# Seven products on eight column tiles in every second gate-and-up pair, with one weight sum per group formed by an accumulating DMA and one more buffer for raw and split weights

## The chip, the cores and the metric

The kernel runs on one core of one Trainium2 chip. The metric is the device time of one execution in microseconds (us). The engines are TensorE (PE, its weight loads PEld), VectorE (DVE), ScalarE (ACT), GpSimd (POOL) and SyncE (SP), which issues nearly all loads. SBUF is the on-chip memory that tiles live in, PSUM the banks that matmuls add up in.

## The reference

A trunk of two layers on 256 tokens with 2048 features, in float32. Each layer has a block of two gated mixers (a causal convolution and an attention with forget gates), a SwiGLU FFN with 5632 hidden columns, and a gated embedding of the layer:

```python
h = rmsnorm(x, norm_mix_g[i]); proj = h @ w_in[i]
glu_in, q, k, v, f_logit, g_conv, g_attn = jnp.split(proj, split_pts, axis=-1)
y_conv = conformer_conv(glu_in, ...)
log_f = jax.nn.log_sigmoid(f_logit + b_forget[i])
y_attn = forgetting_attention(q, k, v, log_f) @ w_attn_out[i]   # scores + C[t] - C[s], causal softmax
x = x + (sigmoid(g_conv) * y_conv + sigmoid(g_attn) * y_attn) @ w_out[i]
gate, up = jnp.split(rmsnorm(x, norm_ffn_g[i]) @ w_gate_up[i], 2, axis=-1)
x = x + (silu(gate) * up) @ w_down[i]
x = x + sigmoid(rmsnorm(x, norm_ple_g[i]) @ w_ple_gate[i]) * (p[i] @ w_ple_proj[i])
```

After the two layers comes a last rmsnorm. Here C is the running sum of log_f over the tokens.

## The kernel before

**Numbers.** A float32 product is made of three matmuls in fp32r: both operands are split into a rounded part and a remainder, and `Sum.add` (L178, L179, L180) adds rounded x rounded, rounded x remainder and remainder x rounded into one PSUM bank. `split` (L139, L140) makes the two parts of a weight half: ScalarE writes the rounded part `h` (a `wh` buffer), VectorE the remainder `l` (a `wl` buffer). `halves` (L299 to L304) does it for activations.

**Tiles.** Activations lie transposed in 16 column tiles of 128 features by 256 tokens. A weight chunk has 512 columns; it comes in groups of four column tiles, each in two halves of 128 x 1024 (512 KB). `fetch` (L131) loads a half on SP into one of `RAWS` = 7 buffers; `wh` and `wl` have 4 buffers each. One half put through `plain` is 12 matmuls with 512 columns: 2 column tiles x 2 token blocks x 3.

**Seven products.** `fast_chunks` takes two weight chunks together, w1 and w2 (for the FFN gate and up). For its first group (or groups, as many as the list `fast` is long), it does not take the 2 x 2 blocks of tokens and column-tile halves by the eight block products but by seven (a form of Strassen's scheme). The activations' combinations are made once by the class `Fast`, on VectorE, for four column tiles. The weights' combinations are made for each pair, out of the four raw halves a11, a12 (of w1) and a21, a22 (of w2): s3 = a11 + a21, then a21 + a22, a11 + a21 and a12 + a11 in place, by `add` (L245) on VectorE. Each of the seven `product`s splits one raw half and is 6 matmuls. p1, q5, q6 and q7 go to their own banks of the pool `ms`, c11, c12 and c21 are shared with the plain halves. The other groups are plain halves; `go` takes the next of them, and so they stand between the products. When the products that make the `u` tiles are done, u1, u4, u3 and u5 are made from the four `ms` banks on ScalarE and VectorE (L260 to L264), and from then on `go` also runs what waits in `turns`, such as transposing the hidden columns of the pair before (`operand`, L313).

**Where it is used.** There are 24 such pairs a layer: 4 for the branch gates, 2 for the output projection, 10 for gate and up (c = 1 to 10; c = 0 is plain), 6 for the down projection in three parts, and 2 for the embedding's gate. All have one group in seven products. In the FFN `norm.fast` holds one `Fast`, and the groups at column tiles 4, 8 and 12 are plain.

**Order.** The program text is given to a scheduler that sets the order on each engine and gives tiles their buffers; each engine then runs its list in order and waits on semaphores. A raw half is fetched when a raw buffer is given back, a split is made when a `wh` and a `wl` buffer are given back by TensorE.

**Other places.** In the attention's `scores`, C[s] is taken off by matmuls that are added to the q k product: with `nsel`, a stack of eight 128 x 128 matrices with one row of -1 each, against `ch` (the running sums in f32; block 0, L706) or `chs` (their two fp32r parts; block 1, L710 and L711). At the start, `warm` issues 10 f32 matmuls on constants, `load_x` brings the first four column tiles in two loads, and `take(0)` scales and splits all four of them before the first weights are split (L159 to L163). POOL makes constants, fills the convolution's margins (L557) and takes the powers of the norms (L425, L446).

Of the kernel before, what the change touches and what calls it, by code (L numbers as in the profile page):

```python
# [35 lines left out]
WARM = 10  # L36
RAWS = 7
# [8 lines left out]
def trunk(ctx, tc, xT, xR, pT, wI, wF, wC, wA, wOut, wGU, wD, wPG, wPP, vec, bF, gF, out):  # L46
# [5 lines left out]
    whs = pool("whs", 4)  # L52
    wls = pool("wls", 4)
    tmps = pool("tmps", 9)
# [13 lines left out]
    def small(n=2):  # L68
        return keep.tile([P, 16], F32, tag="small", name=f"small{next(uid)}", bufs=12)[:, :n]
# [55 lines left out]
    nsel = const.tile([P, H, P], F32R, tag="nsel", name="nsel")  # L125
# [20 lines left out]
    def fetch_first(src, hook):  # L146

        parts = []
        for half in range(2):
# [3 lines left out]
            c = half * 1024  # L153
            if half == 0:
                for k in range(2):
                    nc.scalar.dma_start(raw[:, k, :], src[:, k * 512 : (k + 1) * 512])
                warm()
                hook()
            else:  # L159
                nc.sync.dma_start(raw.rearrange("p k n -> p (k n)"), src[:, c : c + 1024])  # L160
            for k in range(2):
                act.activation(h[:, k, :], raw[:, k, :], AF.Copy)  # L162
                dve.tensor_tensor(l[:, k, :], raw[:, k, :], h[:, k, :].bitcast(F32), op=ALU.subtract)  # L163
# [50 lines left out]
    def fast_chunks(fast, w1, w2, xs, ks, first, to=None, by_block=None):  # L214
# [32 lines left out]
        for g, f in enumerate(fast):  # L247
            a11, a21 = fetch(w1[g][:, :1024]), fetch(w2[g][:, :1024])
            a22, a12 = fetch(w2[g][:, 1024:]), fetch(w1[g][:, 1024:])
            s3 = raws.tile([P, 2, 512], F32, tag="raw", name=f"sum{next(uid)}")  # L250
            product(p1, f(B11), a11)
            add(s3, a11, a21)
# [5 lines left out]
            product(q6, f(T2), a11)  # L258
            if g == len(fast) - 1:
# [177 lines left out]
    def rstd_c(q):  # L437
# [14 lines left out]
        rb = keep.tile([P, S], F32, tag="rb", name=f"rb{next(uid)}", bufs=1)  # L452
# [13 lines left out]
    def take(q, lo=0, hi=4):  # L466
        for k in range(lo, hi):
            if k % 2 == 0:
                o = pair(F32R)
                norm.tiles[4 * q + k], norm.tiles[4 * q + k + 1] = o[:, 0, :], o[:, 1, :]  # L470
            norm.xs[4 * q + k] = by_blocks(norm.tiles[4 * q + k])
            halves(
                norm.tiles[4 * q + k], xin[q].rearrange("p a b -> p (a b)")[:, k * S : (k + 1) * S],
                norm.gain(4 * q + k),
            )

    load_x(0, 0, 2)
    nc.sync.dma_start(vecs[:, :KD], vec[:, :KD])
# [8 lines left out]
    def hook():  # L487
        load_x(0, 2, 4)
        take(0)
# [9 lines left out]
    def rest(q):  # L499
        def go():  # L500
            take(q)
# [18 lines left out]
    for i in range(L):  # L520
# [61 lines left out]
        wf = keep.tile([P, KD, H], F32, tag="wf", name=f"wf{next(uid)}", bufs=1)  # L582
        nc.sync.dma_start(wf, wF[i].rearrange("p (k h) -> p k h", h=H))
        wfc = keep.tile([P, KD, 2, H], F32R, tag="wfc", name=f"wfc{next(uid)}", bufs=1)
# [3 lines left out]
        ch = keep.tile([P, S], F32, tag="ch", name=f"ch{next(uid)}", bufs=1)  # L588
# [54 lines left out]
        def running_sums():  # L643
# [4 lines left out]
            act.activation(ch, pc[:, :S], AF.Copy)  # L648
            halves(chs, ch)
# [18 lines left out]
        if i == 0:  # L668
            for h in range(H):
                dve.tensor_scalar(nsel[:, h, :], ones, ident[:, h : h + 1], -1.0, op0=ALU.mult, op1=ALU.mult)  # L670
# [24 lines left out]
        def scores(hd):  # L695
            st = {}

            def sc():
                q, kt = qT[hd], kT[hd]
                pr = []  # L700
                for b in range(2):
# [3 lines left out]
                    if b == 0:  # L705
                        pe.matmul(  # L706
                            ps[:, :n], lhsT=nsel[:, hd, :].bitcast(F32), rhs=ch[:, :n], start=False, stop=True
                        )
                    else:
                        pe.matmul(ps[:, :S], lhsT=nsel[:, hd, :], rhs=chs[:, S:], start=False, stop=False)  # L710
                        pe.matmul(ps[:, :S], lhsT=nsel[:, hd, :], rhs=chs[:, :S], start=False, stop=True)  # L711
# [161 lines left out]
        norm = Norm(g_ffn, fast=1)  # L873
# [170 lines left out]
```

## Time and profile before

| | before |
|---|---|
| median of 3 runs | 2839.4 us (2838.63 to 2839.59) |
| the profiled execution | 2838.76 us |
| its span, first to last instruction | 2836.7 us |
| mean granted clock of TensorE | 0.998 |
| matmuls of L178, L179, L180, each | 3552 into `mm`, 416 into `ms` |
| HBM read | 538.91 MB, 191 GB/s over the span |
| raw halves loaded for gate and up | 352 of 512 KB |

Lines of the costliest groups are read so: line, engine, operation, what it writes and reads, shapes, count, then busy time and the mean of one instruction in ns, then the engine's idle time before them and what ended most of it. Names are those of the program with the numbers left out: `raw` and `sum` are raw halves, `wh` and `wl` split ones, `mm` and `ms` PSUM banks, `pair` tiles of activations. A line of the timeline has the start, the length, the engine and the line, and the number of instructions merged into it. A line of the waits has who waited for whom, the sum in us, how often, and the longest.

### The profile page before, as it was taken

What the parts mean: (1) busy time and instruction counts of PE and PEld (TensorE: products, weight loads), DVE (VectorE), ACT (ScalarE), POOL (GpSimd) and SP (SyncE); (2) the same over time, 40 slices, a digit from 0 to 9 for tenths busy, and PEclk for the clock granted to TensorE, in tenths of its full rate; (3) what the DMA queues carried; (4) which work ended last, traced back from release to release, by engine and by line L of the source; (5) the groups of instructions that cost most, each with busy time, mean ns of one, the idle gap of its engine ahead of it and who ended that gap; (6) DMA issues with size and microseconds to landing.
All of it is one profiled execution on the core that took longest, in us unless ns stands there. A gap on an engine that the chain in (4) does not pass through costs nothing.

```text
span 2836.7 us, 34661 instructions
## 1 busy us (share of the span) xinstructions
PE 2816.3 (99%) x12744; PEld 2330.0 (82%) x12744; DVE 2342.3 (83%) x2992; ACT 1560.0 (55%) x1883; POOL 9.9 (0%) x41
## 2 busy tenths in 40 slices
PE   9999999999999999999999999999999999999998
PEld 7888888888888888888788888888888888888886
DVE  6998877868888888888869988678688888888877
ACT  6445745555555545556644466455555555455565
POOL 0000000000000000000000000000000000000000
PEclk9999999999999999999999999999999999999999
DMA  7554555565555556555555545555555556556563
GB/s 284 189 183 156 180 200 193 174 203 186 192 200 202 191 198 202 194 191 199 189 175 188 180 154 190 197 192 178 193 195 194 198 193 210 184 199 207 177 222 128
DMA packets 150074, 543.28 MB, mean 192 GB/s; under 512 B 16912, under 2 KB 17168, under 8 KB 149648
## 3 DMA queue, kind: packets, MB, share of 16 engines
q1 hardware_dynamic: 149040, 539.50, 56.3%
q8 instruction: 99, 1.62, 0.2%
q10 hardware_dynamic: 864, 1.57, 0.2%
q14 instruction: 71, 0.58, 0.1%
HBM read 538.91 MB, written 2.10 MB: 191 GB/s over the span
## 4 chain that ended last, share of the span: by engine, by line
PE 93%; DVE 5%; issue 1%; ACT 1%; DMA 0%; SPq 0%; POOLq 0%; POOL 0%; DVEq 0%; ACTq 0%
PE mm L180 27%; PE mm L179 27%; PE mm L178 27%; PE ms L178 3%; PE ms L180 3%; PE ms L179 3%; DVE wl L140 2%; DVE pair L544 2%; PE ms L313 2%; PE ms L704 0%; ACT wh L139 0%; PE ms L740 0%; DVE raw L245 0%; DMA pair<-in_xT_dram 0%; DVE pair L780 0%
## 5 line engine op out<-in xcount | busy, mean ns | idle before, releaser
L139 ACT ACTIVATE wh<-raw 128x1024 fp32r<-128x1024 f32 x1110 | 1175.9, 1061 | 1113.4 <-PE mm L180 909.5
L140 DVE TENSOR_TENSOR wl<-raw,wh 128x1024 fp32r<-128x1024 f32 x1110 | 1344.2, 1222 | 443.9 <-ACT wh L139 430.1
L178 PE MATMUL mm<-wh,pair 128*128 128x512 f32 x3552 | 1390.4, 392 | 4.2 <-ACT wh L162 2.3
L180 PE MATMUL mm<-wh,pair 128*128 128x512 f32 x3552 | 1384.4, 390 | 0.8 <-DVE pair L301 0.8
L179 PE MATMUL mm<-wl,pair 128*128 128x512 f32 x3552 | 1384.6, 390 | 0.4 <-DVE wl L140 0.3
L180 PEld LDWEIGHTS mm<-wh,pair 128*128 128x128 f32 x3552 | 667.0, 188 | 140.8 <-DVE pair L301 1.7
L178 PEld LDWEIGHTS mm<-wh,pair 128*128 128x128 f32 x3552 | 667.0, 188 | 140.0 <-ACT wh L139 2.7
L179 PEld LDWEIGHTS mm<-wl,pair 128*128 128x128 f32 x3552 | 667.7, 188 | 137.8 <-DVE wl L140 1.3
L544 DVE SCALAR_TENSOR_TENSOR pair<-pair,vecs,pair 128x256 f32<-128x256 f32 x480 | 202.7, 481 | 0.0
L245 DVE TENSOR_TENSOR raw<-raw,raw 128x1024 f32<-128x1024 f32 x144 | 175.9, 1222 | 2.7 <-DMA raw<-in_wD_dram 0.3
L178 PE MATMUL ms<-wh,pair 128*128 128x512 f32 x416 | 162.8, 391 | 1.0 <-ACT pair L975 1.0
L180 PE MATMUL ms<-wh,pair 128*128 128x512 f32 x416 | 162.0, 389 | 0.0
L179 PE MATMUL ms<-wl,pair 128*128 128x512 f32 x416 | 161.9, 389 | 0.0
L178 PEld LDWEIGHTS ms<-wh,pair 128*128 128x128 f32 x416 | 78.1, 188 | 17.9 <-ACT pair L975 1.8
L180 PEld LDWEIGHTS ms<-wh,pair 128*128 128x128 f32 x416 | 78.1, 188 | 16.3
L179 PEld LDWEIGHTS ms<-wl,pair 128*128 128x128 f32 x416 | 78.1, 188 | 16.1
L139 ACT ACTIVATE wh<-sum 128x1024 fp32r<-128x1024 f32 x48 | 50.9, 1061 | 67.0 <-PE mm L180 67.0
L140 DVE TENSOR_TENSOR wl<-sum,wh 128x1024 fp32r<-128x1024 f32 x48 | 58.6, 1220 | 11.6 <-ACT wh L139 11.6
L245 DVE TENSOR_TENSOR sum<-raw,raw 128x1024 f32<-128x1024 f32 x48 | 58.8, 1224 | 2.3 <-DMA raw<-in_wGU_dram 1.0
L288 DVE TENSOR_TENSOR tmp<-mm,tmp 128x512 f32<-128x512 f32 x80 | 51.4, 682 | 2.7 <-PE mm L180 2.7
L245 DVE TENSOR_TENSOR tmp<-tmp,mm 128x512 f32<-128x512 f32 x80 | 51.4, 680 | 0.0
L245 DVE TENSOR_TENSOR tmp<-tmp,ms 128x512 f32<-128x512 f32 x80 | 51.1, 681 | 0.0
(179 smaller groups left out, 1122.8 us busy)
## 6 DMA issues: line engine op xcount, KB each, us to landing
raw<-in_wGU_dram SPq DMA_DIRECT2D x352, 512.0 KB, 4.3
raw<-in_wI_dram SPq DMA_DIRECT2D x287, 512.0 KB, 4.0
raw<-in_wD_dram SPq DMA_DIRECT2D x176, 512.0 KB, 3.9
raw<-in_wOut_dram SPq DMA_DIRECT2D x64, 512.0 KB, 3.7
raw<-in_wPG_dram SPq DMA_DIRECT2D x64, 512.0 KB, 4.2
raw<-in_wA_dram SPq DMA_DIRECT2D x32, 512.0 KB, 4.6
raw<-in_wC_dram SPq DMA_DIRECT2D x32, 512.0 KB, 4.5
raw<-in_wPP_dram SPq DMA_DIRECT2D x8, 512.0 KB, 5.6
```

Source lines behind the costliest of these rows:

```text
L139: act.activation(h, raw, AF.Copy)
L140: dve.tensor_tensor(l, raw, h.bitcast(F32), op=ALU.subtract)
L178: pe.matmul(self.t, lhsT=xh, rhs=wh, start=start, stop=False)
L179: pe.matmul(self.t, lhsT=xh, rhs=wl, start=False, stop=False)
L180: pe.matmul(self.t, lhsT=xl, rhs=wh, start=False, stop=self.left == 0)
L245: add = lambda o, a, b: dve.tensor_tensor(o, a, b, op=ALU.add)
L288: dve.tensor_tensor(u, c.t, u, op=ALU.subtract)
L313: pe.transpose(pt[:, kk * S + b * P : kk * S + (b + 1) * P], src(b)[:, c : c + P], ident)
L544: dve.scalar_tensor_tensor(cv[c], u[c][:, j : j + S], w, cv[c], op0=ALU.mult, op1=ALU.add,)
```

## The change

In the FFN the norm holds two `Fast` operands. A pair with odd c uses both: eight of its 16 column tiles go through seven products, and the groups at 8 and 12 are plain. A pair with even c uses the first only, as before. In all pairs s3 is no longer added on VectorE: a11's half is loaded a second time into s3's buffer, and a DMA issued by POOL adds a21's half from HBM onto it. Inside a group the products and plain halves stand in another order. The raw buffers become 8, the split ones 5 each; to make room, the scratch tiles (`tmps`) become 8 and also hold `wf`, `wfc` and `pin`, and some small tiles share or go.

In `scores`, both blocks use the two fp32r parts `chs`, and the matrix with the row of -1 is one column of a negated identity, `nident`, repeated 128 times in the access pattern; `nsel` and `ch` go. At the start there are 20 warm-up matmuls, the first column tile is loaded by itself, the gains (`vecs`) are loaded by POOL, and each of the first column tiles is scaled just before the weights that it meets are split.

```diff
-WARM = 10
-RAWS = 7
+WARM = 20
+RAWS = 8
...
-    whs = pool("whs", 4)
-    wls = pool("wls", 4)
-    tmps = pool("tmps", 9)
+    whs = pool("whs", 5)
+    wls = pool("wls", 5)
+    tmps = pool("tmps", 8)
...
             for k in range(2):
+                take(0, 2 * half + k)
                 act.activation(h[:, k, :], raw[:, k, :], AF.Copy)
...
             a22, a12 = fetch(w2[g][:, 1024:]), fetch(w1[g][:, 1024:])
-            s3 = raws.tile([P, 2, 512], F32, tag="raw", name=f"sum{next(uid)}")
+            s3 = fetch(w1[g][:, :1024])
+            nc.gpsimd.dma_start(s3.rearrange("p k n -> p (k n)"), w2[g][:, :1024], accum_op=ALU.add)
             product(p1, f(B11), a11)
-            add(s3, a11, a21)
             add(a21, a21, a22)
             product(q5, f(M1), a21)
             go()
             product(q7, f(T3), s3)
             add(a11, a11, a21)
             product(q6, f(T2), a11)
+            product(c21, f(N4X), a22)
+            if len(left) > 2 * len(ks):
+                go()
+            product(c11, f(B21), a12)
+            add(a12, a12, a11)
             if g == len(fast) - 1:
...
                 state["quiet"] = False
-                go()
-            product(c21, f(N4X), a22)
             if len(left) > 2 * len(ks):
                 go()
-            product(c11, f(B21), a12)
-            if g == 0 and len(left) > 2 * len(ks):
-                go()
-            add(a12, a12, a11)
             product(c12, f(B22), a12)
...
-    load_x(0, 0, 2)
-    nc.sync.dma_start(vecs[:, :KD], vec[:, :KD])
+    nc.gpsimd.dma_start(vecs[:, :KD], vec[:, :KD])
+    load_x(0, 0, 1)
...
     def hook():
+        load_x(0, 1, 2)
         load_x(0, 2, 4)
-        take(0)
...
-        wf = keep.tile([P, KD, H], F32, tag="wf", name=f"wf{next(uid)}", bufs=1)
+        wf = tmps.tile([P, KD, H], F32, tag="tmp", name=f"wf{next(uid)}")
...
-            act.activation(ch, pc[:, :S], AF.Copy)
-            halves(chs, ch)
+            halves(chs, pc[:, :S])
...
-                    if b == 0:
-                        pe.matmul(
-                            ps[:, :n], lhsT=nsel[:, hd, :].bitcast(F32), rhs=ch[:, :n], start=False, stop=True
-                        )
-                    else:
-                        pe.matmul(ps[:, :S], lhsT=nsel[:, hd, :], rhs=chs[:, S:], start=False, stop=False)
-                        pe.matmul(ps[:, :S], lhsT=nsel[:, hd, :], rhs=chs[:, :S], start=False, stop=True)
+                    row = nident[:, hd : hd + 1].to_broadcast([P, P])
+                    pe.matmul(ps[:, :n], lhsT=row, rhs=chs[:, S : S + n], start=False, stop=False)
+                    pe.matmul(ps[:, :n], lhsT=row, rhs=chs[:, :n], start=False, stop=True)
...
-        norm = Norm(g_ffn, fast=1)
+        norm = Norm(g_ffn, fast=2)
...
-                    up = fast_chunks(norm.fast, w1, w2, norm.xs, (4, 8, 12), gate)
+                    nf = 1 + c % 2
+                    up = fast_chunks(norm.fast[:nf], w1, w2, norm.xs, (4, 8, 12)[nf - 1 :], gate)
...
-                pin = keep.tile([P, 2, S], F32, tag="pin", name=f"pin{i}", bufs=1)
+                pin = tmp().rearrange("p (k s) -> p k s", k=2)
```

More of the change, by code (lines that the diff above doesn't have):

```diff
@@ L464, in load_x, with take @@
         )
[L466 to L474, printed above, removed]
[L475 to L478 removed]
+    def take(q, k):
+        if k % 2 == 0:
+            o = pair(F32R)
+            norm.tiles[4 * q + k], norm.tiles[4 * q + k + 1] = o[:, 0, :], o[:, 1, :]
+        to = norm.tiles[4 * q + k]
+        halves(to, xin[q].rearrange("p a b -> p (a b)")[:, k * S : (k + 1) * S], norm.gain(4 * q + k))
+        norm.xs[4 * q + k] = by_blocks(to)
+    nc.gpsimd.dma_start(vecs[:, :KD], vec[:, :KD])
+    load_x(0, 0, 1)
     def warm():
@@ L500, in go @@
         def go():
-            take(q)
+            for k in range(4):
+                take(q, k)
             load_x(q + 1) if q < 3 else None
```

16 lines of the change are left out of this document (6 added, 10 removed).

## The prediction

> **What bounds the kernel now.** I read the page first (engine shares, chain, costliest groups), then what TensorE waits for, then one gate-and-up pair of the FFN, where the change puts its new products. All of it is the profiled execution of before: 2838.76 us, of which the span is 2836.7, so 2.1 us lie around it; the median of the runs, 2839.4, is 0.6 higher, and the sum below is made against 2838.8.
>
> ```profile
> span 2836.7 us, 34661 instructions
> PE 2816.3 (99%) x12744; PEld 2330.0 (82%) x12744; DVE 2342.3 (83%) x2992; ACT 1560.0 (55%) x1883; POOL 9.9 (0%) x41
> PE 93%; DVE 5%; issue 1%; ACT 1%; DMA 0%; SPq 0%; POOLq 0%; POOL 0%; DVEq 0%; ACTq 0%
> L139 ACT ACTIVATE wh<-raw 128x1024 fp32r<-128x1024 f32 x1110 | 1175.9, 1061 | 1113.4 <-PE mm L180 909.5
> L140 DVE TENSOR_TENSOR wl<-raw,wh 128x1024 fp32r<-128x1024 f32 x1110 | 1344.2, 1222 | 443.9 <-ACT wh L139 430.1
> L245 DVE TENSOR_TENSOR sum<-raw,raw 128x1024 f32<-128x1024 f32 x48 | 58.8, 1224 | 2.3 <-DMA raw<-in_wGU_dram 1.0
> ```
>
> The reader is to see that the kernel is TensorE's: 99% busy, 93% of the chain. The splitters wait for it and not the other way: ScalarE's rounding (L139) idles 909.5 us for a matmul to give back a split tile, and VectorE's remainder (L140) idles behind that rounding. A busy PE can hide pauses, so its waits and its pace come next.
>
> ```profile
> PE mm L178 <- ACT wh L162: 2.3, 1, 2.3
> PE mm L178 <- ACT wh L139: 1.8, 3, 1.2
> PE ms L485 <- POOL ones L105: 1.2, 1, 1.2
> ...
> 1500.06 0.39 PE L179 MATMUL mm<-wl,pair 128*128 128x512 f32 x1
> ...
> 1501.42 0.39 PE L179 MATMUL mm<-wl,pair 128*128 128x512 f32 x1
> ...
> 694.18:737.26 43.08, 43.08 (x196) 35.74 (x195) 34.67 (x36) 22.73 (x25) 0.00 (x0) 1.00 0.57 195
> 2264.90:2308.00 43.10, 43.10 (x196) 35.76 (x195) 36.84 (x41) 24.55 (x27) 0.00 (x0) 1.00 0.58 193
> ...
> L313 PE MATMUL ms<-ident,tmp 128*128 128x128 f32 x8 | 1.0, 272 | 0.0
> ...
> L261 DVE TENSOR_TENSOR tmp<-tmp,ms 128x512 f32<-128x512 f32 x1 | 0.7, 681 | 0.0
> ```
>
> TensorE's largest waits together are about 5 us, two thirds of that in the first 8 us. From 1500.06 to 1501.42 there are six steps of one matmul: 1.36 / 6 = **0.227 us** for 128x512. A pair before is 186 such matmuls (7 products of 6, 12 plain halves of 12) and 8 transposes of about 1.0 us together: 186 x 0.227 + 1.0 = 43.2 against 43.08 measured from one pair's end to the next. So a pair holds nothing but matmuls, and a matmul taken out is worth its 0.227 us as long as the splits keep up. Columns of the window rows are length, then busy time (and count) of PE, PEld, DVE, ACT, POOL, granted clock, DMA share and GB/s: VectorE has 34.67 to 36.84 us of work in a pair, 80 to 85%.
>
> **The change, part by part.**
>
> *Seven products on eight column tiles, c = 1, 3, 5, 7, 9 of each layer.* The second group of four column tiles costs 7 x 6 = 42 matmuls instead of 4 x 12 = 48. Six saved, ten pairs: 60 x 0.227 = **-13.6 us**. An odd pair should take 43.1 - 1.4 = 41.7 us.
>
> *What the odd pair needs from VectorE.* Three splits more (22 instead of 19) and two additions more (six instead of four, since the sum s3 leaves in both groups): 5 x 1.22 = 6.1 us, so 34.67 + 6.1 = 40.8 to 36.84 + 6.1 = 42.9 us, against 41.7 of TensorE. The even pair loses one addition: 33.4 to 35.6 of 43.1. Over two pairs 74.2 to 78.5 of 84.8 us (88 to 93%). VectorE fits on the mean and is level with TensorE in the odd half, where the fifth wh and wl buffers carry it: I take 0 for stalls. If this cover is gone, the tightest place decides: after the last plain half of the second group come five products back to back, 5 x 1.36 = 6.8 us on TensorE, with five splits, two additions and four updates like L261 (0.68 us) on VectorE, 11.3 us. The 4.5 us difference must come from split tiles made ahead (four ahead, as the next fence shows, and in this stretch worth 1.36 to 2.72 us each). ScalarE gains 3 x 1.06 us in 41.7 and has room.
>
> *The sum s3 by DMA, 58 groups.* Out go 48 additions of 1.22 us on VectorE, which TensorE did not wait for: 0 gained. In come 58 loads on SP and 58 accumulating loads on POOL, 512 KB each: 2 x 58 x 0.524 = 60.8 MB.
>
> ```profile
> 722.58 1.23 DVE L245 TENSOR_TENSOR sum<-raw,raw 128x1024 f32<-128x1024 f32 x1
> ...
> 736.07 1.28 DVE L288 TENSOR_TENSOR tmp<-mm,tmp 128x512 f32<-128x512 f32 x2
> ...
> 738.59 1.22 DVE L140 TENSOR_TENSOR wl<-sum,wh 128x1024 fp32r<-128x1024 f32 x1
> ...
> 736.55 1.06 ACT L139 ACTIVATE wh<-sum 128x1024 fp32r<-128x1024 f32 x1 [1.66 <-PE mm L180]
> ...
> q1 hardware_dynamic: 149040, 539.50, 56.3%
> raw<-in_wGU_dram SPq DMA_DIRECT2D x352, 512.0 KB, 4.3
> pair<-in_xT_dram SPq DMA_DIRECT2D x3, 512.0 KB, 9.6
> ```
>
> Bandwidth holds: 56.3% for 539.5 MB becomes about 63%; an odd pair moves 20 halves, 10.5 MB in 41.7 us, 252 GB/s against 195. What matters is lateness. Today s3's slot is free at 722.58 and its rounding starts at 736.55, when TensorE has just begun the pair (its last result of the pair before is read at 736.07) with four split tiles ahead. In those 14.0 us now go a load (4.3 us) and the accumulating load, so the latter may take 9.7 us before anything is late, and about 15 before TensorE is, as the four tiles ahead hold 1.36 + 1.36 + 2.72 us or more. With eight raws and five split buffers both ends move earlier by about one tile. The second group of an odd pair is tighter: its s3 gets a slot at the split of the second plain half, and from there to its own split lie four products and two halves, 4 x 1.36 + 2 x 2.72 = 10.9 us of TensorE (8 x 1.22 = 9.8 of VectorE). Less 4.3, the accumulating load may take 5.5 to 6.6 us, and about 8 before TensorE stands, since the tiles ahead are also wanted by the five products. No accumulating DMA is in the trace; the nearest rows are 4.3 and, for the slowest transfers of that size, 9.6 us. I take 6, beside the 4.3, because both move the same bytes and only the second reads the tile too: **0**. At 9.6 us it would be (9.6 - 8) x 10 = +16. The page "DMA: Bandwidth & Descriptors" of the Trainium skill, section "Anatomy of one DMA — SWDGE (gpsimd) path", fits a transfer issued by GpSimd by 2.0 us plus bytes over 436 GB/s, an estimate of 3.2 us here; by it the sum would be the same, and no run yet shows it.
>
> *Queues.* SP issues 58 more loads and never leads the chain (SPq 0%). On POOL the powers of the norms and of the convolution's norm (L425, L446) and the memsets of L557 queue behind an accumulating load that waits for its first load. Their readers come a projection or more later, except L446, which a matmul waits for in the background work: 0 to 4.3 us, once a layer; I take **+0.5**.
>
> *Scores.* The f32 matmul pair with nsel in block 0 becomes two fp32r ones with chs; block 1 stays two.
>
> ```profile
> 200.15 0.49 PE L704 MATMUL ms<-pair,pair 128*128 128x128 f32 x2
> 200.47 0.39 PE L706 MATMUL ms<-ch,nsel 128*128 128x128 f32 x2
> 200.69 0.60 PE L704 MATMUL ms<-pair,pair 128*128 128x256 f32 x2
> 200.94 0.47 PE L710 MATMUL ms<-chs,nsel 128*128 128x256 f32 x1
> 201.25 0.28 PE L711 MATMUL ms<-chs,nsel 128*128 128x256 f32 x1
> 201.36 0.39 PE L178 MATMUL mm<-wh,pair 128*128 128x512 f32 x1
> ```
>
> By starts, L706 costs 200.69 - 200.47 = 0.22 us, and the fp32r pair L710, L711 costs 201.36 - 200.94 = 0.42 at twice the columns. The step from fp32r to f32 also costs: L704 takes 0.32 for 128 columns behind fp32r and 0.25 for 256 behind f32, so about 0.1. Per head the rise lies between 0 (half the columns, half the time) and 0.2 + 0.1 = 0.3 us, and 16 heads give 0 to +4.8. As the 0.42 seems to be mostly the change of type and of weights, I take 0.22 a head: **+3.5**.
>
> *Start.*
>
> ```profile
> 1.20 4.44 PE L485 MATMUL ms<-ones 128*128 128x128 f32 x20 [1.20 <-POOL ones L105]
> 7.97 0.73 PE L178 MATMUL mm<-wh,pair 128*128 128x512 f32 x2 [2.33 <-ACT wh L162]
> ...
> 10.56 0.63 PE L178 MATMUL mm<-wh,pair 128*128 128x512 f32 x1
> 10.99 0.63 PE L179 MATMUL mm<-wl,pair 128*128 128x512 f32 x1
> ...
> 5.34 0.91 ACT L303 ACTIVATE pair<-pair,vecs 128x256 fp32r<-128x256 f32 x2 [2.12 <-DMA vecs<-in_vec_dram]
> ```
>
> After the pause from 5.64 to 7.97 the matmuls start 0.43 us apart until about 11.8, some 6 of them, 1.3 us lost. Twenty more warm-up instructions fill that pause. Against it, vecs comes by POOL, behind its memsets, perhaps 2 us later, while ScalarE needs one scaled tile before the first weights instead of four (3 x 0.46 us less). Between -1.5 and +1.7; I take **-0.5**.
>
> *The rest at 0.* The second fast operand of the FFN norm (some 2 us more on each of VectorE and ScalarE, twice) lies beside the second output pair, where two sums leave VectorE. The freed nsel builds were idle filling. The eight tmps now also hold wf, wfc and pin; the slots that these loads need were last read a projection earlier, so SP should not stop. If it did, one load and one split (4.3 + 2.3 us) at four places, 26 us, would show as SP waiting.
>
> *Sum:* -13.6 + 0.5 + 3.5 - 0.5 = -10.1; 2838.8 - 10.1 = **2828.7 us**.
>
> **Rivals.**
>
> *A, the forecast* (2824 to 2833.7): TensorE stays saturated. For it: a pair without a gap, and 88 to 93% on VectorE over two pairs. Against: level loads in the odd pair.
>
> *B, the odd pairs stall*: VectorE becomes the bound in them, or their second s3 is a little late. Each loses 0.5 to 1.6 us, ten times 5 to 16: 2834 to 2845. For it: 42.9 us of VectorE in 41.7, and the 4.5 us at the five products. Against: VectorE idles over 6 us in the pair before.
>
> *C, slower*: the accumulating load takes over 9.6 us behind 250 GB/s of other loads, and TensorE waits for q7 in the second group of every odd pair. From about 9.6 us on the loss passes the gain; at 12 it is (12 - 8) x 10 = +40, 2869; past 15 all 58 groups stall, +58 us for each us. For it: one 512 KB transfer did take 9.6. Against: the median is 4.3 at 57% load. One way to it, 0.04 of C's 0.13: POOL can't prepare the transfer while VectorE is in a long run of splits.
>
> ```profile
> 708.36 4.72 DVE L140 TENSOR_TENSOR wl<-raw,wh 128x1024 fp32r<-128x1024 f32 x4
> ```
>
> With 4.7 us of waiting on top of 6 it takes 10.7: (10.7 - 8) x 10 = +27, 2856. The page "SBUF — State Buffer" of the Trainium skill, section "SBUF: two separate sides", has such a rule, against this change: descriptors of a GpSimd DMA wait while VectorE holds a shared port in a two-port mode. Its section "Who interferes with whom" only infers that an operation on two tensors, as here, leaves the descriptors free; no run here shows either.
>
> *D, better than the sum*: fp32r at 128 columns costs nothing more and the start gains fully: 2838.8 - 13.6 - 1.5 = 2823.7, or a little below as the old waits leave.
>
> **How the numbers follow.** A 0.60, B 0.21, C 0.13, D 0.06. About 0.2%, 5.7 us, is what a measurement of this kernel can tell from no change: faster is below 2833.7, slower above 2845.1. Faster holds A and D, 0.66; within, B, 0.21; slower, C, 0.13. The range takes in A, B and most of D: 2822.5 to 2845.
>
> **What would show it.** Right: 11844 matmuls with 512 columns; odd pairs of 41.7 us and even ones of 43.1 from up's last product to the next; "sum" gone from VectorE; TensorE's waits near 10 us in all; rows of the scores' L710 form at block 0, 0.3 to 0.4 us a pair. Wrong: TensorE waiting for ScalarE's rounding of the sum (C, or late s3), for L140 in odd pairs (B); SP waiting for a tmp; the first 512-column matmul later than 10 us.

## The result

| kernel | median us (range, executions) | against before, 95% interval |
|---|---|---|
| before | 2839.4 (2838.6 to 2839.8, 6) | |
| changed | 2859.8 (2858.4 to 2861.9, 6) | 1.0074 [1.0063, 1.0085] |

The changed kernel is 20.4 us slower; 2828.7 was forecast, and the range ended at 2845. The matmuls are as announced: 60 with 512 columns fewer, 11844. The first view is the page of the changed kernel: spans, engines, queues, the chain of waits, and its costliest groups beside the rows quoted of before (lines moved by one: L140, L141, L246 were L139, L140, L245; the product's matmuls are L179 to L181).

```profile
span 2857.9 us, 34978 instructions
PE 2818.6 (99%) x12704; PEld 2320.6 (81%) x12704; DVE 2350.7 (82%) x3000; ACT 1576.1 (55%) x1916; POOL 60.6 (2%) x100
...
q1 hardware_dynamic: 157392, 569.91, 59.0%
q0 software_dynamic: 8384, 30.42, 6.1%
...
PE 14%; DVE 2%; DMA 1%; issue 1%; ACT 0%; POOLq 0%; POOL 0%; DVEq 0%; ACTq 0%
...
L140 ACT ACTIVATE wh<-raw 128x1024 fp32r<-128x1024 f32 x1188 | 1237.6, 1058 | 1150.8 <-PE mm L181 754.7
L141 DVE TENSOR_TENSOR wl<-raw,wh 128x1024 fp32r<-128x1024 f32 x1188 | 1425.1, 1221 | 427.6 <-ACT wh L140 423.9
...
L246 DVE TENSOR_TENSOR raw<-raw,raw 128x1024 f32<-128x1024 f32 x174 | 212.7, 1222 | 32.9 <-DMA raw<-in_wD_dram 17.1
```

PE is busy 2.3 us more than before with 60 matmuls less. A busy PE holds pauses here: a matmul in front of which weights come late is shown as a longer one (0.50 us instead of 0.39 in the rows of c = 3 below). The 59% of q1 carries 569.9 MB, so 0.104% for each MB; q0, the accumulating transfers that POOL issues, takes 0.20% for each MB (run 4 shows why). The chain's 14% only says that it could be followed back over a small part of the span; it can't be set against the 93% of before. What TensorE and ScalarE wait for in the changed kernel says more (columns: us in total, times, longest):

```profile
PE mm L180 <- DVE wl L141: 10.6, 18, 1.1
PE mm L179 <- ACT pair L303: 5.6, 1, 5.6
...
ACT wh L140 <- DVE raw L246: 140.0, 65, 5.4
...
ACT wh L140 <- DMA raw<-in_wGU_dram: 75.3, 27, 5.4
```

TensorE has two new waits: one of 5.6 us for a scaled activation (the start), and 18 for a remainder. Behind the second stand ScalarE's waits for VectorE's additions (140.0 us, 21.7 before) and, 75.3 us in 27 waits, for weights of gate and up.

For the whole sum I cut both traces at the starts of the 512-column matmuls, counted in program order, and took each stage's length from its first to the next stage's first:

| stage, both layers together | before to changed, us | forecast |
|---|---|---|
| to the end of the first gate projection (end at 97.9, now 105.5) | +7.6 | -0.5 |
| the ten odd pairs | +8.9 | -13.6 |
| the pairs c = 2 | +4.6 | 0 |
| second half of the branch gates, with the scores | +2.3 | +3.5 |
| last part of the down projection | +2.1 | 0 |
| embedding's gate and end | -3.7 | 0 |
| all else | -0.6 | 0 |
| span | +21.2 | |

An odd pair should have lost 1.36 us. None did: the nearest, c = 9 of the first layer, lost 0.9, and c = 3 there went from 42.2 to 44.8 us. So some 22.5 us of stalls (8.9 + 13.6) stand in the odd pairs, and that and the start are the failure.

**One odd pair read closely.** First the source view of L252, the 58 accumulating loads (who waited for them, us, times; then the time to landing). Then, for the second group of c = 3, the transfers' rows, SP's and POOL's, with the median us to landing; and the time lines of SP, POOL, ScalarE, VectorE and TensorE (start, length, engine, line; in brackets the idle time before it and what ended it).

```profile
ACT wh L140: 67.1, 20
...
DMA to landing us min/median/max: 5.6/8.1/9.8
```

```profile
raw<-in_wGU_dram SPq DMA_DIRECT2D x1, 512.0 KB, 5.1
...
raw<-in_wGU_dram POOLq DMA_DIRECT2D x1, 512.0 KB, 9.1
```

```profile
818.93 0.33 SPq L134 DMA_DIRECT2D raw<-in_wGU_dram  x1
...
824.68 0.85 POOL L252 DMA_DIRECT2D raw<-in_wGU_dram  x1 [20.31 <-issue]
...
833.91 2.96 ACT L140 ACTIVATE wh<-raw 128x1024 fp32r<-128x1024 f32 x3 [5.07 <-DMA raw<-in_wGU_dram]
...
835.00 4.63 DVE L141 TENSOR_TENSOR wl<-raw,wh 128x1024 fp32r<-128x1024 f32 x4 [4.90 <-ACT wh L140]
...
835.61 0.39 PE L179 MATMUL ms<-wh,pair 128*128 128x512 f32 x1
836.29 0.50 PE L180 MATMUL ms<-wl,pair 128*128 128x512 f32 x1 [0.29 <-DVE wl L141]
...
842.12 0.50 PE L179 MATMUL mm<-wh,pair 128*128 128x512 f32 x1 [0.29 <-ACT wh L140]
843.38 0.50 PE L180 MATMUL mm<-wl,pair 128*128 128x512 f32 x1 [0.76 <-DVE wl L141]
```

The slot's first load is issued at 818.93 and takes 5.1 us; POOL issues the accumulating load at 824.68, and it lands 9.1 us later at 833.8. ScalarE, which takes its tiles in order, idles 5.07 us in front of it, VectorE then 4.90 us. From 818.93 to 833.8 the sum has taken 14.9 us, where the prediction had worked out 10.9 us between slot and split; in all ten second groups it is 12.9 to 14.9, 14.1 in the median. TensorE runs on from the tiles ahead until 835.6, and then loses 0.45 us, 0.44 us and 1.03 us (steps of 0.68, 0.67 and 1.26 in place of 0.227), 1.9 of the pair's 4.0, of which the rows call only 1.3 idle; most of the rest is one more such step, 1.27 us too long, at 847.7. The 4.9 us that VectorE lost come back as late splits behind the sum, among the products that the prediction had called the tightest place.

### The profile page after: what moved, and what is told of

Read it like the earlier page. It is cut to its first block, busy times and chain, and to the rows that moved or that the text cites. A ratio compares the mean times of both kernels' runs of the same rounds, so it can differ in the third digit from the quotient of the medians.

```text
span 2857.9 us, 34978 instructions
## 1 busy us (share of the span) xinstructions
PE 2818.6 (99%) x12704; PEld 2320.6 (81%) x12704; DVE 2350.7 (82%) x3000; ACT 1576.1 (55%) x1916; POOL 60.6 (2%) x100
## 3 DMA queue, kind: packets, MB, share of 16 engines
q0 software_dynamic: 8384, 30.42, 6.1%
## 5 line engine op out<-in xcount | busy, mean ns | idle before, releaser
L140 ACT ACTIVATE wh<-raw 128x1024 fp32r<-128x1024 f32 x1188 | 1237.6, 1058 | 1150.8 <-PE mm L181 754.7
L141 DVE TENSOR_TENSOR wl<-raw,wh 128x1024 fp32r<-128x1024 f32 x1188 | 1425.1, 1221 | 427.6 <-ACT wh L140 423.9
L179 PE MATMUL mm<-wh,pair 128*128 128x512 f32 x3452 | 1354.1, 392 | 9.4 <-ACT pair L303 5.6
L180 PE MATMUL mm<-wl,pair 128*128 128x512 f32 x3452 | 1348.8, 391 | 11.2 <-DVE wl L141 10.6
L181 PE MATMUL mm<-wh,pair 128*128 128x512 f32 x3452 | 1345.7, 390 | 0.0
L179 PEld LDWEIGHTS mm<-wh,pair 128*128 128x128 f32 x3452 | 648.9, 188 | 144.9 <-ACT wh L140 6.6
L181 PEld LDWEIGHTS mm<-wh,pair 128*128 128x128 f32 x3452 | 648.8, 188 | 135.5 <-DVE pair L304 0.8
L246 DVE TENSOR_TENSOR raw<-raw,raw 128x1024 f32<-128x1024 f32 x174 | 212.7, 1222 | 32.9 <-DMA raw<-in_wD_dram 17.1
L179 PE MATMUL ms<-wh,pair 128*128 128x512 f32 x496 | 194.4, 392 | 2.0 <-ACT wh L140 1.7
L180 PE MATMUL ms<-wl,pair 128*128 128x512 f32 x496 | 193.6, 390 | 1.1 <-DVE wl L141 1.1
L181 PE MATMUL ms<-wh,pair 128*128 128x512 f32 x496 | 193.1, 390 | 0.0
L179 PEld LDWEIGHTS ms<-wh,pair 128*128 128x128 f32 x496 | 93.1, 188 | 23.6 <-ACT wh L140 3.0
L181 PEld LDWEIGHTS ms<-wh,pair 128*128 128x128 f32 x496 | 93.1, 188 | 19.4
L246 DVE TENSOR_TENSOR tmp<-tmp,mm 128x512 f32<-128x512 f32 x80 | 51.9, 680 | 0.0
L246 DVE TENSOR_TENSOR tmp<-tmp,ms 128x512 f32<-128x512 f32 x80 | 51.1, 680 | 0.0
L252 POOL DMA_DIRECT2D raw<-in_wGU_dram x30 | 25.6, 854 | 816.4 <-DVE wl L141 289.2
L399 ACT ACTIVATE tmp<-xt 128x512 f32<-128x512 f32 x56 | 34.8, 623 | 14.1 <-DVE xt L862 8.4
L862 DVE TENSOR_TENSOR xt<-xt,tmp 128x512 f32<-128x512 f32 x64 | 41.1, 684 | 0.0
```

Of the source, the lines that this page charges most:

```text
L140: act.activation(h, raw, AF.Copy)
L141: dve.tensor_tensor(l, raw, h.bitcast(F32), op=ALU.subtract)
L179: pe.matmul(self.t, lhsT=xh, rhs=wh, start=start, stop=False)
L180: pe.matmul(self.t, lhsT=xh, rhs=wl, start=False, stop=False)
L181: pe.matmul(self.t, lhsT=xl, rhs=wh, start=False, stop=self.left == 0)
L246: add = lambda o, a, b: dve.tensor_tensor(o, a, b, op=ALU.add)
```

## The experiments

The theory after this reading: the two transfers of a *second* s3 do not fit into the time between its slot and its split (lateness); and the start is lost to vecs on POOL. The rivals: VectorE's load in the odd pair stalls them whatever s3 does; accumulating as such or POOL hold the engines up; the scores or the new order cost it. The ratio is against before, which was run beside each.

| run | median us | ratio, 95% interval |
|---|---|---|
| vecs_on_sp | 2854.0 | 1.0054 [1.0039, 1.0069] |
| one_fast | 2845.9 | 1.0026 [1.0017, 1.0036] |
| second_sum_on_vector | 2834.7 | 0.9986 [0.9976, 0.9995] |
| plain_on_pool | 2839.6 | 1.0003 [0.9993, 1.0012] |
| vecs_sp_second_vector | 2827.4 | 0.9956 [0.9939, 0.9973] |
| vecs_sp_sum_loaded_first | 2860.4 | 1.0074 [1.0059, 1.0089] |
| vecs_sp_all_sums_vector | 2827.0 | 0.9955 [0.9941, 0.9970] |
| vecs_sp_every_pair | 2834.2 | 0.9986 [0.9976, 0.9995] |
| vecs_sp_second_four_bufs | 2864.6 | 1.0093 [1.0078, 1.0108] |
| vecs_sp_seven_raws | 2910.2 | 1.0258 [1.0241, 1.0276] |
| vecs_sp_all_vector_c1_one | 2824.8 | 0.9951 [0.9934, 0.9967] |

### 1. The start: vecs back on SP

```diff
-    nc.gpsimd.dma_start(vecs[:, :KD], vec[:, :KD])
     load_x(0, 0, 1)
+    nc.sync.dma_start(vecs[:, :KD], vec[:, :KD])
```

> The changed kernel with one line moved: the gains of the first tiles (vecs) are loaded by SP again, behind the first column tile, instead of by POOL. In the changed kernel the first 512-column matmul starts at 14.19 us (7.97 before) and the GLU stage takes 91.3 us (90.0 before), 7.6 us lost together. Theory (the gains' transfer and the place that the scheduler gives to its readers is the whole loss of the start): first matmul near 8 us, 2859.8 - 7.6 = 2852 us. Rival (the split loads, the twenty more warm-up matmuls or the scaling between the splits cost it): first matmul still after 11 us, 2856 us or more. Nothing in the FFN should move.

The transfer's row (KB, us to landing) in the changed kernel, in vecs_on_sp and in before:

```profile
vecs<-in_vec_dram POOLq DMA_DIRECT2D x1, 8.0 KB, 6.5
```

```profile
vecs<-in_vec_dram SPq DMA_DIRECT2D x1, 8.0 KB, 3.3
```

```profile
vecs<-in_vec_dram SPq DMA_DIRECT2D x1, 8.0 KB, 4.0
```

The start of the changed kernel, from the time lines of POOL, ScalarE and TensorE, and a window row (its last three numbers: granted clock, DMA share, GB/s); then of vecs_on_sp:

```profile
2.89 0.74 POOL L474 DMA_DIRECT2D vecs<-in_vec_dram  x1
...
10.21 1.06 ACT L140 ACTIVATE wh<-raw 128x1024 fp32r<-128x1024 f32 x1 [0.18 <-DMA raw<-in_wI_dram]
...
12.68 1.06 ACT L140 ACTIVATE wh<-raw 128x1024 fp32r<-128x1024 f32 x1 [0.18 <-DMA raw<-in_wI_dram]
13.64 1.69 ACT L303 ACTIVATE pair<-pair,vecs 128x256 fp32r<-128x256 f32 x4
...
14.19 0.80 PE L179 MATMUL mm<-wh,pair 128*128 128x512 f32 x1 [5.57 <-ACT pair L303]
...
16.46 0.63 PE L180 MATMUL mm<-wl,pair 128*128 128x512 f32 x1
16.89 0.63 PE L181 MATMUL mm<-wh,pair 128*128 128x512 f32 x1
...
13.70:20.50 6.80, 6.28 (x14) 4.49 (x15) 2.87 (x6) 2.02 (x6) 0.00 (x0) 0.50 1.03 422
```

```profile
4.59 0.51 ACT L303 ACTIVATE pair<-pair,vecs 128x256 fp32r<-128x256 f32 x1 [1.37 <-DMA vecs<-in_vec_dram]
...
7.58 0.48 PE L179 MATMUL mm<-wh,pair 128*128 128x512 f32 x1
7.90 0.39 PE L180 MATMUL mm<-wl,pair 128*128 128x512 f32 x1
8.13 0.40 PE L181 MATMUL mm<-wh,pair 128*128 128x512 f32 x1
```

On POOL the 8 KB land at 9.4 us (2.89 + 6.5). That alone is 4.2 us later than in before (issued at 1.24, 4.0 to landing); the rest is order: on ScalarE the first scaling stands *behind* the roundings of 10.21 to 12.68, of later weights, and starts at 13.64, and TensorE idles 5.57 us. It then runs at steps of 0.43 us (16.46 to 16.89), and the window row says why: the granted clock (the share of its full clock that TensorE gets) is 0.50 from 13.7 to 20.5 us. In before it is 0.50 from 8.7 to 12.1 us, behind a pause of 2.33 us; in vecs_on_sp nowhere at the start. On SP the first product starts at 7.58 and soon runs at 0.23 us a step, and the first projection ends at 96.1 instead of 105.5: 9.4 us. The median moved by 5.8 only, and the span by 2.3: the profiled execution (2857.3) is the slowest of its four, and its odd pairs are 8.3 us longer in sum than the changed kernel's, where nothing in the FFN should have moved. The accumulating transfers are as slow (median 8.2), but load and sum of a second group together take 13.9 to 16.0 us, 15.0 in the median against 14.1; ten times that is about the difference. Why they are slower here stays open.

### 2. Without the second group: one_fast

```diff
-        norm = Norm(g_ffn, fast=2)
+        norm = Norm(g_ffn, fast=1)
...
-                    nf = 1 + c % 2
+                    nf = 1
```

> The changed kernel with seven products on four column tiles in all gate-and-up pairs, as before the change (the FFN norm has one such operand), and everything else of the change kept: sums by DMA, more buffers, scores, start. Theory (late: the second group's sum lands too late in the odd pairs, and its lateness reaches into the pair behind it): all pairs at 43.1 us, the FFN's 15.3 us of loss gone, 2859.8 - 15.3 = 2844.5 us; the first groups' sums never stop TensorE. Rival (the accumulating transfers cost TensorE something everywhere): pairs above 43.3 us and 2850 us or more.

All pairs are as in before to 0.04 us (43.1; 42.2 for c = 3 and 7), although every first group still has its sum by DMA, with a median of 7.9 us to landing. So a sum of 8 us is in time in a first group and too late only in a second one. The median is 6.4 us over before, and the span of the trace 6.8: the start (+6.4), branch gates (+1.0 and +1.4), the last part of the down projection (+0.9) and the embedding's gate (-1.5 and -1.1).

### 3. The second sum on VectorE: second_sum_on_vector

```diff
-            s3 = fetch(w1[g][:, :1024])
-            nc.gpsimd.dma_start(..., w2[g][:, :1024], accum_op=ALU.add)
+            if g == 0:
+                s3 = fetch(w1[g][:, :1024])
+                nc.gpsimd.dma_start(..., w2[g][:, :1024], accum_op=ALU.add)
+            else:
+                s3 = raws.tile([P, 2, 512], F32, tag="raw", name=f"sum{next(uid)}")
             product(p1, f(B11), a11)
+            if g > 0:
+                add(s3, a11, a21)
```

> The changed kernel, but in the second group of the odd gate-and-up pairs (ten groups of 58) the sum s3 is added on VectorE as before the change; all other sums stay by DMA. Theory (late): the accumulating transfer of the second group takes 8.0 to 9.3 us where 5.5 to 6.6 were to spare, and ScalarE idles 3.5 to 5.4 us in front of it; without it odd and even pair together fall from 87.1 to 90.2 us (89.9 in the median of those seen) to about 84.8 to 85.5, and the kernel to 2831 to 2838 us. Rival (work: the odd pair has more splits and additions than VectorE and ScalarE can do): VectorE gets 1.2 us more in each odd pair, so the pairs stay where they are or grow, 2859 us or more.

The windows of the pair c = 3, of the changed kernel and then of this one (length, busy time and count of PE, PEld, DVE, ACT, POOL, clock, DMA share, GB/s):

```profile
812.45:857.28 44.83, 42.28 (x181) 33.49 (x181) 38.02 (x39) 22.98 (x24) 1.70 (x2) 1.00 0.68 207
```

```profile
810.05:850.85 40.80, 40.80 (x182) 33.79 (x181) 39.00 (x40) 23.34 (x24) 0.85 (x1) 1.00 0.65 203
```

VectorE has one addition *more* to do (39.00 against 38.02 us) and the pair is 4.0 us shorter. All ten odd pairs take 41.7 us (c = 3 and 7: 40.8), 1.33 to 1.40 less than in before. The mechanism of seven products is worth what was forecast, and VectorE's load in the odd pair doesn't bind: ten second sums by DMA cost 25.2 us (2859.8 - 2834.7).

### 4. The same transfers without accumulating: plain_on_pool

```diff
-            nc.gpsimd.dma_start(..., w2[g][:, :1024], accum_op=ALU.add)
+            nc.gpsimd.dma_start(..., w2[g][:, :1024])
```

> The changed kernel with the 58 transfers on POOL not accumulating: the half of w2 lands over the half of w1 in the buffer of s3, so s3 is not the sum. The order on every engine is that of the changed kernel; the same bytes come from HBM. If it is the accumulation that makes the transfer long (8.1 us in the median from issue to landing, against 4.7 for a load on SP): about 4.5 to 5.5 us to landing, the stalls in the odd pairs shrink to under 1 us, 2835 to 2842 us. If it is the traffic of the burst or the issue by POOL: still 7 us or more, and 2855 us or more.

The order of instructions is the same on every engine, and the bytes, the queue and the wait too. The source view of L252, and the queue's row:

```profile
ACT wh L140: 29.8, 12
...
DMA to landing us min/median/max: 3.3/5.7/7.8
...
q0 software_dynamic: 8384, 30.42, 3.2%
```

Accumulating makes a transfer of 512 KB on POOL 8.1 instead of 5.7 us; on SP a half takes 4.7. It also doubles the time of the DMA engines: the same 30.42 MB on the same queue take 3.2% of the span instead of 6.1%, or 0.105% for each MB, about what SP's loads take. With 5.7 the odd pairs come to 41.7 but for c = 3 (42.5 and 41.6) and c = 7 (41.9 and 42.0), and the kernel is 20.2 us faster than the changed one. So 2.4 us of landing time, over a threshold, are worth 20 us.

### 5. Both repairs, and what the DMA sum is worth

vecs_sp_second_vector joins 1 and 3; vecs_sp_all_sums_vector has no sum by DMA at all:

```diff
-            s3 = fetch(w1[g][:, :1024])
-            nc.gpsimd.dma_start(..., w2[g][:, :1024], accum_op=ALU.add)
+            s3 = raws.tile([P, 2, 512], F32, tag="raw", name=f"sum{next(uid)}")
             product(p1, f(B11), a11)
+            add(s3, a11, a21)
```

> The changed kernel with vecs loaded by SP and the second group's sum in the odd pairs added on VectorE. Theory (the two losses are separate and these are all of it): the start ends some 1.8 us ahead of before at the end of the GLU stage (96.1 against 97.9 us in the run with vecs on SP), the ten odd pairs stay at 41.7 us, and the kernel comes to 2834.7 - 9.4 = 2825.3 us, range 2823 to 2828, below both kernels. If the losses are not separate (an earlier start only moves the wait elsewhere): 2830 us or more.

> The changed kernel with vecs on SP and no sum by DMA at all: every s3 is added on VectorE as before the change, the odd pairs kept. VectorE then has 34.67 + 6 x 1.22 = 42.0 us to 36.84 + 7.3 = 44.2 us of work in an odd pair, against 41.7 us of TensorE, and 34.7 to 36.8 of 43.1 in the even one. Theory (work matters only where VectorE's sum over two pairs passes TensorE's): 76.7 to 81 of 84.8 us over two pairs, so the buffers nearly cover it; odd pairs lose 0 to 1 us each, 2824 to 2834 us. Rival (the sums by DMA are needed for the seven products to pay): odd pairs lose 1.4 us or more each, 2839 us or more.

2827.4 and 2827.0: the sums by DMA in the first groups bring nothing and cost nothing, as one would expect of work taken from an engine that TensorE isn't waiting for. 33 us of the changed kernel's time were its two late things.

### 6. The sum's transfers first: vecs_sp_sum_loaded_first

```diff
+            s3 = fetch(w1[g][:, :1024])
+            nc.gpsimd.dma_start(..., w2[g][:, :1024], accum_op=ALU.add)
             a11, a21 = fetch(w1[g][:, :1024]), fetch(w2[g][:, :1024])
             a22, a12 = fetch(w2[g][:, 1024:]), fetch(w1[g][:, 1024:])
-            s3 = fetch(w1[g][:, :1024])
-            nc.gpsimd.dma_start(..., w2[g][:, :1024], accum_op=ALU.add)
```

> The changed kernel with vecs on SP, and all sums still by DMA, but in each group the two transfers of s3 are issued ahead of those of a11, a21, a22 and a12 instead of behind them. Theory (late: what stops the odd pairs is the time from the second group's first transfer to its use): the load of s3 gets the first raw buffer that comes free in the group instead of the fifth, some 8 us earlier, which covers the 8 to 9 us of the accumulating transfer; odd pairs at 41.7 to 42 us, kernel 2824 to 2829 us. Rival (the burst of loads beside an accumulating transfer is what stops the odd pairs, whatever the order): the delay moves to a11 or a21, pairs above 43 us, 2840 us or more.

The theory's total was missed, and the rival's (2840 us or more) came: 6.4 us above vecs_on_sp (2854.0). The part that the theory speaks of came: the odd pairs c = 1, 5 and 9 are at 41.7 us and c = 7 at 40.8 and 41.1 (c = 3 takes 46.7 and 46.3, as against 44.3 and 46.8). But the order holds for every group, and branch gates (+8.3 and +7.4) and the embedding's gate (+7.0) now stall. TensorE's waits there:

```profile
PE ms L719 <- DVE tmp L712: 10.5, 2, 5.7
PE mm L180 <- DVE wl L141: 7.7, 2, 4.1
```

Our reading, which no run shows apart: a buffer held from the first fetch of a group to its third product is one less for the loads of a11 to a12, so the lateness moved. Part of the price is the clock: it was granted at 0.50 in five stretches, 27.3 us in all, in these places and in c = 3; vecs_on_sp has none.

### 7. Two groups in every pair: vecs_sp_every_pair

As vecs_sp_second_vector, with `nf = 2` for all c from 1 on.

> The kernel with vecs on SP and the second sum on VectorE, but all pairs c = 1 to 10 put eight column tiles through seven products, not only the odd ones: twenty pairs of 41.7 us at best, another 60 x 0.227 = 13.6 us of matmuls less. VectorE has 34.67 + 3 splits + 3 additions = 42.0 us and up to 44.2 in each pair, with no lighter pair behind it. If work then decides, each pair takes 42 to 44 us, VectorE's time, and the kernel comes to 2825 to 2850 us, no better than with every second pair; if the buffers and VectorE's overlap of successive instructions are enough, 2812 to 2818 us.

60 matmuls less than vecs_sp_second_vector and 6.8 us slower in the median (1.7 in the span). c = 4 and 8 gain in full, 41.7 us; c = 5 and 9 take 43.6 to 43.7, and the part of the down projection behind c = 2 is 1.4 and 4.2 us longer (the second with 3.4 us at a granted clock of 0.50). The windows of c = 4 and c = 5, columns as above:

```profile
841.17:882.90 41.73, 41.73 (x190) 34.61 (x188) 40.34 (x44) 25.63 (x28) 0.85 (x1) 1.00 0.73 234
882.90:926.57 43.67, 42.58 (x190) 34.49 (x189) 42.93 (x44) 25.96 (x29) 0.86 (x1) 1.00 0.67 214
```

VectorE is busy 83.3 of the 85.4 us of both, and its 42.93 in c = 5 are more than TensorE's 41.7. Here its load does bind; a pair with one group between gives it back what the odd pair takes.

### 8. Four split buffers instead of five

As vecs_sp_second_vector, with four `wh` and four `wl`.

> As vecs_sp_second_vector (2827.4 us; odd pairs 41.7), but four wh and four wl buffers instead of five, as in the kernel before. The prediction put it that the fifth split buffers carry the odd pairs over the stretch with 11.3 us of VectorE work against 6.8 us of TensorE. If so, each of the ten odd pairs loses about one split tile's worth, 1.36 us, here: 13.6 us, about 2841, and TensorE waits for VectorE's remainder in odd pairs. Rival: four tiles ahead do, since the mean load of VectorE leaves room: 2827 to 2830, odd pairs 41.7.

37.2 us more, over twice what was expected. The odd pairs lose 1.8 to 1.9 us each (c = 3 and 7: 2.7 to 4.3), 23.6 together; the branch gates lose 5.8, the embedding's gate 4.3. Three stretches of 3.4 us at a granted clock of 0.50, one in the branch gates of each layer and one in the c = 3 of 4.3 us, are part of this. TensorE's waits:

```profile
PE mm L180 <- DVE wl L141: 14.8, 10, 2.0
PE mm L179 <- ACT wh L140: 6.0, 9, 1.3
```

Ten waits for a remainder, in the first layer one in each of the five odd pairs. So the fifth buffers carry the odd pairs, as the prediction said, and other places too, which it had not counted.

### 9. Seven raw buffers instead of eight

As vecs_on_sp, all sums by DMA, with RAWS = 7.

> As vecs_on_sp (2854.0 us, all sums by DMA), but seven raw buffers instead of eight. If the odd pairs stall because the two transfers of the second s3 (about 15 us together) do not fit between the time its buffer comes free and its split, one buffer fewer takes about one product or half plain half (1.4 to 2.7 us) off that time, and each of ten odd pairs gets longer by that: 14 to 27 us more, 2868 to 2881, and first groups may begin to be late as well. Rival: the stall is not set by when the buffer comes free (but, say, by the transfers' mere share of the DMA queues): within 3 us of 2854.

56 us more than vecs_on_sp, twice the expectation's upper end, with the sign and place that lateness demands: the odd pairs are 30.9 us longer in sum (3.1 each; 1.4 to 2.7 had been expected), and c = 2 another 8.3. The transfers did not get slower (median 7.5 us against 8.2); what shrank is the time that they have. The expectation had left out the clock, which was granted at 0.50 in seven stretches in c = 2, 3, 5 and 7, 27.3 us in all (vecs_on_sp: none). Half speed costs at most half of that, 13.6 us. The first of them, as a window row:

```profile
702.92:709.73 6.81, 5.72 (x14) 3.92 (x15) 4.64 (x5) 4.02 (x6) 0.00 (x0) 0.50 0.79 271
```

### 10. What is left at c = 2

In the kernels with two groups in c = 1, c = 2 is 1 to 4 us too long (5 and 7 with seven raw buffers); in one_fast it isn't. The time line of VectorE around its start (691.3) in vecs_sp_all_sums_vector, first and last of the six instructions that make the down projection's first operand, and the addition behind them:

```profile
684.75 0.75 DVE L341 TENSOR_TENSOR pair<-pair 128x256 f32<-128x256 f32 x2
...
689.50 1.21 DVE L351 TENSOR_TENSOR pair<-pair,pair 128x1024 fp32r<-128x1024 f32 x1
690.63 1.21 DVE L246 TENSOR_TENSOR raw<-raw,raw 128x1024 f32<-128x1024 f32 x1
```

In before these stand at 664.1 to 670.0, over 20 us ahead of the next pair. With two groups the `u` tiles are made later, and what waits in `turns` behind them runs at the end of c = 1, just ahead of the splits for c = 2. The test leaves c = 1 at one group:

```diff
-                    nf = 1 + c % 2
+                    nf = 1 + (c % 2 and c > 1)
```

> As vecs_sp_all_sums_vector (2827.0 us), but the pair c = 1 of each layer has one group in seven products, so that eight pairs instead of ten have two. In that run the pair c = 2 takes 45.5 and 45.2 us where the even pairs otherwise take 43.1. One reading: the first operand of the down projection is made in c = 1 (L341, L351, about 4.1 us of VectorE), and with two groups in c = 1 it comes only at the pair's end, ahead of the additions and splits that c = 2 begins with (684.8 to 690.7 us there, against 664.1 to 670.0 in before, 20 us ahead of that end). If so, c = 1 takes 43.1 us (1.36 more) and c = 2 takes 43.1 (2.4 and 2.1 less): 1.8 us less in all, about 2825.2. Rival: c = 2 is late for another reason (the raw and split buffers that two groups in any pair before leave) and stays at 45: 2.7 us more, about 2829.7.

c = 1 takes 43.1 us, c = 2 takes 43.1, and the median is 2824.8 (2825.2 expected). Against the rival speak the other even pairs too: in vecs_sp_all_sums_vector c = 4, 6, 8 and 10 also stand behind a pair with two groups and take 43.1 to 43.4 us. Twelve more matmuls, 2.2 us less. This is the fastest kernel of the study, 0.9951 of before.

## Why the prediction was wrong

**Seven products, -13.6: right as a mechanism.** Wherever s3 was in time (runs 3 and 5), the odd pairs took 41.7 us, as forecast.

**The odd pair's need from VectorE, 0: right, with the reason given.** Odd and even pair together were put at 74.2 to 78.5 us of VectorE; the windows of c = 1 and 2 of the changed kernel, each from its first product to the next pair's, hold 36.35 + 37.99 = 74.3. The odd pair holds less than was forecast and the even one more, as some of the work falls behind the pair's end:

```profile
658.79:702.58 43.79, 42.76 (x189) 34.47 (x188) 36.35 (x39) 25.13 (x28) 1.70 (x2) 1.00 0.69 206
702.58:748.40 45.82, 44.15 (x195) 35.62 (x194) 37.99 (x40) 24.58 (x26) 0.85 (x1) 1.00 0.74 239
```

Run 8 shows that the cover, the fifth split buffers, carries it; run 8's expectation priced that cover at 13.6 us, and the odd pairs alone lost 23.6. Rival B's first mechanism (VectorE as the bound) falls by run 3, and stands where every pair has two groups (run 7).

**The sum by DMA, 0: this step failed, in the size of one term.** The text had the structure: 10.9 us from slot to split in the second group, 4.3 for the first load, so 5.5 to 6.6 for the accumulating one and about 8 until TensorE stands. Then it took 6, the nearer to the plain load, and priced everything by that. It measured 8.1 in the median and 8.0 to 9.3 in the ten second groups, and the first load before it took 4.2 to 5.3 instead of 4.3, so load and sum took 12.9 to 14.9 instead of 10.3. So the point was passed. The price beyond it was also too low: by (8 to 9.3 - 8) x 10 = 0 to 13 us the sum would have come to at most 2841.7, within the range; the stalls were 22.5 us in the odd pairs by the trace and 25.2 us by run 3. The rule counted only the time until the sum's own product; VectorE's idle time comes back as late splits in the products behind it. Rival C (0.13) named this cause with a threshold of 9.6, which was too high; rival B's second clause (a second s3 "a little late", to 2845) had the cause at too low a price.

**The accumulating transfer at 3.2 us, and rival C's way to it.** The estimate from the Trainium skill's page "DMA: Bandwidth & Descriptors", section "Anatomy of one DMA — SWDGE (gpsimd) path", was wide of both: 5.7 us plain and 8.1 accumulating were measured beside some 200 GB/s of other loads, and the measurement decides. The rule of the Trainium skill's page "SBUF — State Buffer", section "SBUF: two separate sides", that descriptors wait while VectorE is in a two-port mode, isn't decided: the plain transfers on POOL were faster beside the same VectorE work, so 2.4 us of the 8.1 are the accumulation, and no run took VectorE's splits away.

**Start, -0.5: wrong, +7.6.** The prediction put vecs "perhaps 2 us later" (4.2 measured) and its list of signs had "the first 512-column matmul later than 10 us", which came (14.19). What it left out is the order on ScalarE: the scaling, whose data came late, was placed late in the list, behind roundings that nothing needed yet, and the pause of 5.57 us brings 6.8 us at a granted clock of 0.50, twice what before had. The other half of the term was right: with vecs on SP the first projection ends 1.8 us ahead of before (96.1 against 97.9).

**Scores, +3.5: wrong, about 0.** By starts, the changed pair L701, L702 at 128 columns:

```profile
207.93 0.31 PE L701 MATMUL ms<-chs,nident 128*128 128x128 f32 x1
208.07 0.27 PE L702 MATMUL ms<-chs,nident 128*128 128x128 f32 x1
208.18 0.65 PE L699 MATMUL ms<-pair,pair 128*128 128x256 f32 x2
```

208.18 - 207.93 = 0.25 us against the 0.22 of the one f32 matmul: 0.5 us in 16 heads, the lower end, half the columns in about half the time. Counted from each start to the next one, all matmuls of the scores (L704 to L711, now L699 to L702) take 18.1 us where before they took 18.2, so the +2.3 of their stage comes from elsewhere. D's half of this was right.

**Queues on POOL, +0.5:** TensorE's waits show none for the norms' powers. **The rest at 0:** no load into a tmp made SP wait; unforeseen were c = 2 (+4.6, explained by run 10) and the branch gates (+2.3), embedding (-3.7) and last down part (+2.1). Branch gates and embedding are also so in runs 2 and 5, so they don't belong to the sums by DMA or the second group. In the branch gates it is mostly one step of 1.25 us instead of 0.23 in each layer (at 310.81 and 1727.44), a wait for ScalarE's rounding; which of the changes in order or buffers makes it stays open.

## What to carry to other kernels

Before moving an addition into a DMA, ask whether the path waits for the engine that it leaves; here it did not, so the move could only lose. A step with a threshold ("in time up to 8 us") is not priced at its likeliest duration but by the chance of passing the point and by the whole delay that then runs through the in-order engines behind it. And a buffer more on such a pipeline can be worth more than the work saved: one split buffer was 37 us, one raw buffer 56 us (beside the late sums by DMA; without them it wasn't tried), sixty matmuls 14.

## What was not expected of the hardware

- A DMA of 512 KB on POOL takes 5.7 us plain and 8.1 accumulating (medians of 58 each). Only the accumulating one takes twice the time of the DMA engines: 0.20% of the span for each MB, against 0.105% for the plain one and 0.104% for SP's loads.
- 8 KB by POOL took 6.4 to 7.5 us to landing in the kernels that load vecs so, by SP 3.3 to 4.0; they weren't issued at the same moment, so how much of this is the queue isn't shown.
- Pauses of TensorE cost time once more behind them. Behind the pause of 5.57 us at the start the granted clock was 0.50 for 6.8 us (steps of 0.43 instead of 0.23), behind the 2.33 us of before for 3.4. Short pauses in a row seem to do it too: in vecs_sp_second_vector three steps of 0.95 to 1.06 us from 693.23 on, with no idle time over 0.68 us, were followed by 3.4 us at 0.50 (the row below), and in vecs_sp_every_pair three of 0.95 to 1.17 us from 2142.91 on likewise.

```profile
696.44:699.83 3.39, 3.39 (x11) 2.68 (x11) 3.33 (x3) 0.77 (x2) 0.00 (x0) 0.50 0.82 277
```
